# A mixture-of-experts layer on one core: the sum in two tensors of half the columns, and gate and up weights with two rows to a partition

## The chip, the cores and the metric

The kernel runs on one core of a Trainium2 chip. The metric is the device time of one execution in microseconds (us). The core's engines work side by side, each through its own instructions in order, and wait for each other by semaphores: TensorE (PE; its weight loads are listed apart as PEld), VectorE (DVE), ScalarE (ACT), GpSimd (POOL) and SyncE (SP, which here issues DMAs). Sixteen DMA engines move data between DRAM and the on-chip memory SBUF; TensorE writes its results to PSUM.

## The reference

One decoder layer for 1024 tokens of width 1024: sparse attention and a chunked gMLP side by side, merged, projected and added to the input, and then a mixture of 32 experts. Only the last part bears on the change:

```python
# comb[t, e]: weight of expert e for token t, two experts of one group per token
y = jnp.zeros_like(h)
for e in range(N_EXPERTS):
    he = jax.nn.silu(h @ w_gate[e]) * (h @ w_up[e])     # 1024 -> 256, twice
    y = y + comb[:, e:e + 1] * (he @ w_down[e])         # 256 -> 1024
```

The result is the residual plus `y`, normalised by its root mean square and scaled by `final_norm_g`. All data are float32.

## The kernel before

Up to some 815 us the kernel normalises, projects, attends, merges (`merge`) and routes. The merged residual is written to the DRAM tensor `acc` of 1024 x 1024 floats, in pieces of 128 rows and 512 columns (L1046); the normalised tokens go to the DRAM tensor `h2d`.

The mixture of experts runs over 28 units, in an order fixed when the program is built. Six experts have a fixed place, the others are ordered by their load at run time. A unit is one expert, with up to 128 tokens (three heavily loaded ones have a second, half-size list in the same unit), or a duo: two lightly loaded experts with 64 tokens each. For each unit:

- GpSimd gathers its tokens from `h2d` (L1472) into one of three SBUF pages, whose tiles are called `h` and `g` in the trace: one token on a partition, 1024 columns.
- TensorE transposes them in eight pieces of 128 columns (L1488 in `tokens`, L1500 in `tokens_duo`; output `xt`). The gathered rows are the stationary operand, the identity is the moving one. ScalarE copies the result out (`xh` or, for a duo, `xs`); for a unit that isn't a duo VectorE computes the low part `xl`.
- TensorE multiplies with gate and up weights, eight pieces of 128 rows with gate and up side by side in 512 columns (`gate_up`, L148 to L150 and L1567, L1568; `gate_up_duo`, L1514; output `gu`). A unit that isn't a duo has its weights split into a high part (`wh`, ScalarE, L135) and a low part (`wl`, VectorE, L143) and takes three products per piece.
- ScalarE and VectorE make the activation (`kb`), TensorE multiplies with the down weights (output `y` in PSUM, two slots), ScalarE scales it by the routing weight into one of three SBUF pages `y` (L1553).
- GpSimd issues an indirect DMA that adds the page's rows to the tokens' rows of `acc` in DRAM (`scatter`, L1618). There are 31 of these, two for a duo or a unit with a second list. All write the same tensor, so each waits until the one before has landed. The page `y` is free for ScalarE when its scatters have landed.

The last two units, both duos, aren't scattered; their `y` stays in SBUF, and in `finish` TensorE adds it to the output rows by one-hot matrices (`fin`, L1792). Ahead of that, `fg`, the scale of the last norm, is loaded by GpSimd's queue (L1703), held back until the down product of a given unit is issued on TensorE.

Weights come in pages of 512 KB through SyncE's queue: gate and up as two loads of 256 KB per page (L197, in `gu` of the plan), down as one of 512 KB (L203). They are issued ahead of use as pages come free. The order of instructions on each engine is set by the program's scheduler, from the order in the code, data dependences and its own cost model.

`finish` loads `acc` in eight pages `xf` of 128 rows (L1769), adds the kept `fin` (VectorE, L1820 and L1824; for two of the eight TensorE, L1814), squares and sums (ScalarE, L1825), scales (VectorE, L1784) and stores.

Of the kernel before, what the change touches and what calls it, by code (L numbers as in the profile page):

```python
# [21 lines left out]
P = 128  # L22
T = 1024
# [69 lines left out]
class Kern:  # L93
# [64 lines left out]
    def plan(self):  # L158
# [32 lines left out]
        def gu(gets, eng):  # L191
            for j, get in ((j, get) for j in range(4) for get in gets):

                def ld(t, j=j, get=get):
                    wg, wu, _ = get()
                    for z, w in enumerate((wg, wu)):
                        self.nc.sync.dma_start(t[:, :, z * 256 : (z + 1) * 256], w[j * 256 : (j + 1) * 256, :].rearrange("(k p) f -> p k f", p=P))  # L197

                W.append(([P, 2, 512], ld, eng))
# [33 lines left out]
    def expert(self, e):  # L233
        I = self.I
        return lambda: (I["w_gate"][0, e], I["w_up"][0, e], I["w_down"][0, e])

# [699 lines left out]
    def merge(self):  # L936
# [38 lines left out]
        self.acc = self.dram.tile([T, D], F32, name="acc")  # L975
# [55 lines left out]
        def rest(n):  # L1031
# [14 lines left out]
            writes.append((n, self.acc[rows, cs], x1))  # L1046
# [427 lines left out]

    def tokens(self, xg):
# [9 lines left out]
        for q in range(KT // n):  # L1485
            tp = self.ps1([P, n, m], "xt", tag="a")
            for k in range(n):
                self.lastpe = nc.tensor.transpose(tp[:, k, :], xg[:, (q * n + k) * P : (q * n + k + 1) * P], self.ident[:m, :m])  # L1488
# [4 lines left out]
    def tokens_duo(self, xg):  # L1493
# [3 lines left out]
        for q in range(2):  # L1497
            tp = self.ps1([P, 4, P], "xt", tag="a")
            for k in range(4):
                self.lastpe = nc.tensor.transpose(tp[:, k, :], xg[:, (q * 4 + k) * P : (q * 4 + k + 1) * P], self.ident)  # L1500
# [4 lines left out]
    def gate_up_duo(self, x, r, piece):  # L1505
# [3 lines left out]
        for j in range(4):  # L1509
            ws = [piece() for _ in range(2)]  # L1510
            for k in range(2):
                for z in range(2):
                    zs = slice(z * HALF, (z + 1) * HALF)
                    nc.tensor.matmul(pp[zs], lhsT=x[:, 2 * j + k, zs], rhs=ws[z][:, k, :], start=(j + k == 0), stop=(j + k == 4))  # L1514
# [41 lines left out]
    def gate_up(self, x, r, piece):  # L1556

        nc = self.nc
        pp = self.ps1([P, 512], "gu", tag="b")
        half = len(x) == 1  # L1560
        for j in range(4):
            h, l = piece()
            for k in (2 * j, 2 * j + 1):
                if half:

                    if k:
                        nc.tensor.matmul(pp[:HALF], lhsT=x[0][:, k, :HALF], rhs=l[:, k % 2, :], start=False, stop=False)  # L1567
                    nc.tensor.matmul(pp, lhsT=x[0][:, k, :], rhs=h[:, k % 2, :], start=(k == 0), stop=(k == KT - 1))  # L1568
                    if not k:
                        nc.tensor.matmul(pp[:HALF], lhsT=x[0][:, k, :HALF], rhs=l[:, k % 2, :], start=False, stop=False)  # L1570
                else:
                    self.mm3(pp, x[0][:, k, :], x[1][:, k, :], h[:, k % 2, :], l[:, k % 2, :], k == 0, k == KT - 1)
        if not half:
            return self.silu(pp, r)
        else:
            sg = self.small([P, 256], F32, "kb", bufs=self.NKB)
            rows = self.junk.bitcast(F32)
            nc.scalar.activation(rows, pp, AF.Copy, scale=r)
# [267 lines left out]
```

## Time and profile before

| | us |
|---|---|
| median of three runs | 1214.99 |
| lowest, highest | 1214.33, 1216.02 |
| the profiled execution's own time | 1214.61 |
| its span | 1212.9 |
| TensorE busy in it | 1107.7 (91%) |
| VectorE, ScalarE, GpSimd busy | 839.1, 535.4, 307.9 |

The profile is of one execution, and all stretches below are in microseconds from the start of its span. A busy share is an average over stages with different limits: the kernel's 91% on TensorE say nothing of the last 120 us, so the trace is read there by stretches, by what each engine waits for, and by the order of starts on a time line. On a time line, the bracket at a row's end gives how long the engine had been idle before and what it waited for last; no bracket means no idle time. [...]

### The profile page before, as it was taken

The numbers are of one execution on the slowest core, as the hardware profiler recorded it, in microseconds if no ns is written. First come the engines' busy times: TensorE is split into PE (matmuls) and PEld (weight loads), VectorE is DVE, ScalarE is ACT, GpSimd is POOL, SyncE is SP. The second block draws the span as 40 slices with busy tenths as digits, with TensorE's granted clock in tenths as the row PEclk, the third lists the DMA queues.
The fourth block names the chain that finished last, engine by engine and source line by source line (L and its number), as shares of the span: only waits on it lengthen the run. The fifth ranks groups of instructions, "written<-read, shape, count | busy, mean of one in ns | idle before, by whom it ended". The sixth has DMA issues, their size and how long they took to land. (4 is left out here: it accounts for less than half of the span.)

```text
span 1212.9 us, 17018 instructions
## 1 busy us (share of the span) xinstructions
PE 1107.7 (91%) x5714; PEld 875.5 (72%) x5714; DVE 839.1 (69%) x1640; ACT 535.4 (44%) x958; POOL 307.9 (25%) x339
## 2 busy tenths in 40 slices
PE   4999999998999998899999989996989999895684
PEld 3789888887888886789988878875765666573333
DVE  7534889899999997489887961366895754572015
ACT  6424651312222212478776431323885655562123
POOL 5100033340021120044431541222241712131220
PEclk9999999998999998999999999996999999998797
DMA  7301030302422220000006664787999999999835
GB/s 225 88 18 36 18 78 28 102 37 70 122 87 88 86 86 21 18 1 1 2 2 208 222 221 147 278 272 230 288 303 302 341 334 348 323 350 329 265 77 225
DMA packets 147995, 190.29 MB, mean 157 GB/s; under 512 B 16455, under 2 KB 119407, under 8 KB 147906
## 3 DMA queue, kind: packets, MB, share of 16 engines
q1 hardware_dynamic: 134226, 156.84, 39.2%
q0 software_dynamic: 8640, 20.81, 6.9%
q10 hardware_dynamic: 5040, 11.54, 2.5%
q8 instruction: 46, 0.75, 0.3%
q14 instruction: 43, 0.35, 0.1%
HBM read 165.22 MB, written 33.15 MB: 164 GB/s over the span
## 5 line engine op out<-in xcount | busy, mean ns | idle before, releaser
L143 DVE TENSOR_TENSOR wl<-wr,wh 128x1024 fp32r<-128x1024 f32 x156 | 197.1, 1284 | 35.8 <-ACT wh L135 28.0
L552 DVE TENSOR_SCALAR_CACHE_REDUCE junk<-idx,cand 128x384 bf16<-128x384 f32 (+2 forms) x198 | 187.0, 944 | 6.8 <-POOL idx L515 1.0
L148 PE MATMUL pj<-hT,wh 128*128 128x512 f32 (+1 forms) x464 | 179.5, 387 | 2.5 <-ACT wh L135 2.5
L150 PE MATMUL pj<-hT,wl 128*128 128x512 f32 (+1 forms) x464 | 178.3, 385 | 0.0
L149 PE MATMUL pj<-hT,wh 128*128 128x512 f32 (+1 forms) x464 | 177.9, 384 | 0.0
L135 ACT ACTIVATE wh<-wr 128x1024 fp32r<-128x1024 f32 x150 | 154.2, 1056 | 46.2 <-PE pj L149 28.5
L148 PEld LDWEIGHTS pj<-hT,wh 128*128 128x128 f32 x464 | 87.8, 189 | 19.9 <-ACT wh L135 2.7
L150 PEld LDWEIGHTS pj<-hT,wl 128*128 128x128 f32 x464 | 87.6, 189 | 16.8
L149 PEld LDWEIGHTS pj<-hT,wh 128*128 128x128 f32 x464 | 87.7, 189 | 16.5
L892 POOL TENSOR_SCALAR P<-P,pair 128x128 f32<-128x128 f32 (+3 forms) x64 | 47.9, 749 | 88.3 <-DVE pair L891 78.2
L717 POOL TENSOR_TENSOR yt<-yt,sb 128x1024 f32<-128x1024 f32 x8 | 20.1, 2510 | 169.0 <-ACT sb L725 169.0
L725 ACT ACTIVATE sb<-pj 128x512 f32<-128x512 f32 x32 | 19.0, 593 | 99.1 <-PE pj L150 99.1
L148 PE MATMUL gu<-wh,xh 128*128 128x512 f32 x144 | 59.7, 415 | 2.3 <-ACT wh L135 1.6
L149 PE MATMUL gu<-wl,xh 128*128 128x512 f32 x144 | 60.4, 419 | 1.5 <-DVE wl L143 1.2
L150 PE MATMUL gu<-wh,xl 128*128 128x512 f32 x144 | 58.7, 407 | 0.0
L148 PE MATMUL y<-wh,kb 128*128 128x512 f32 (+1 forms) x84 | 37.3, 444 | 19.1 <-ACT y L1553 17.9
L890 ACT ACTIVATE P<-S,pair 128x128 f32<-128x128 f32 (+3 forms) x64 | 47.5, 742 | 15.4 <-DVE pair L884 7.1
L1514 PE MATMUL gu<-wr,xs 128*64 128x512 f32 x224 | 54.2, 600 | 0.0
L512 DVE SCALAR_TENSOR_TENSOR idx<-rl,era,idx 128x384 f32<-128x384 f32 (+5 forms) x42 | 39.8, 947 | 20.1 <-ACT rl L508 18.9
L148 PE MATMUL xo<-wh,m 128*128 128x512 f32 x128 | 51.4, 402 | 2.1 <-ACT m L135 1.7
L1543 DVE SCALAR_TENSOR_TENSOR kb<-gu,era,kb 128x256 f32<-128x256 f32 x19 | 9.2, 482 | 63.8 <-ACT kb L1542 63.8
L508 ACT ACTIVATE rl<-ix 128x384 f32<-128x384 f32 (+5 forms) x48 | 35.8, 760 | 38.8 <-PE ix L503 34.9
(448 smaller groups left out, 2706.4 us busy)
## 6 DMA issues: line engine op xcount, KB each, us to landing
wr<-w_gate SPq DMA_DIRECT2D x128, 256.0 KB, 6.5
wr<-w_up SPq DMA_DIRECT2D x128, 256.0 KB, 6.4
wr<-w_down SPq DMA_DIRECT2D x64, 512.0 KB, 8.1
wr<-w_in SPq DMA_DIRECT2D x33, 512.0 KB, 4.3
x<-x SPq DMA_DIRECT2D x8, 512.0 KB, 8.0
sga<-sb ACTq DMA_DIRECT2D x8, 512.0 KB, 4.4
ybg<-yt POOLq DMA_DIRECT2D x8, 512.0 KB, 3.3
ybr<-ybg SPq DMA_DIRECT2D x8, 512.0 KB, 3.8
```

Source lines behind the costliest of these rows:

```text
L135: return nc.scalar.activation(out, src, AF.Copy)
L143: b = (self.nc.gpsimd if eng in "pq" else self.nc.vector).tensor_tensor(l, src, h.bitcast(F32), ALU.subtract)
L148: nc.tensor.matmul(out, lhsT=sh, rhs=mh, start=start, stop=False)
L149: nc.tensor.matmul(out, lhsT=sh, rhs=ml, start=False, stop=False)
L150: self.lastmm = nc.tensor.matmul(out, lhsT=sl, rhs=mh, start=False, stop=stop)
L508: nc.scalar.activation(r3, ps[:, :nch, :w], AF.Relu)
L512: nc.vector.scalar_tensor_tensor(acc, rl, wv, acc, op0=ALU.mult, op1=ALU.add)
L552: nc.vector.tensor_scalar(junk[:, : (j + 3) * P], self.idx[j + 2][:, : (j + 3) * P], cf[:, j : j + 1], None, op0=op, op1=ALU.add, accum_ou ...
L717: nc.gpsimd.tensor_tensor(yt, yt, sb, ALU.mult)
L890: nc.scalar.activation(p.rearrange("p (c w) -> p c w", c=nch), ps[:, :nch, :w], AF.Exp, bias=mx, scale=-1.0, accum_out=sm[:, 0:1])
L892: nc.gpsimd.tensor_scalar(p, p, sm[:, 1:2], 0.0, op0=ALU.mult, op1=ALU.add)
L1514: nc.tensor.matmul(pp[zs], lhsT=x[:, 2 * j + k, zs], rhs=ws[z][:, k, :], start=(j + k == 0), stop=(j + k == 4))
```

## The change

The change has two parts.

The weights of gate and up: before, piece k of the 1024 input rows were rows 128k to 128k + 127, one to a partition, so that a partition of a load held two rows of 1 KB from two places. Now partition p holds rows 8p to 8p + 7, piece k being the rows 8p + k, and one load brings rows 8p + 2j and 8p + 2j + 1, which are 2 KB in one run in DRAM and in SBUF. To match, the transposes read every eighth column of the gathered rows (`eighth`), and the gate and up matmuls read gate and up in two runs of 256 columns that don't lie side by side.

The sum: `acc` becomes two tensors of 1024 x 512, each scatter becomes two with 512 columns each, and `finish` loads 16 pieces of 256 KB in the place of 8 of 512 KB.

```diff
 # plan: gate and up pages
-                        self.nc.sync.dma_start(t[:, :, z * 256 : (z + 1) * 256], w[j * 256 : (j + 1) * 256, :].rearrange("(k p) f -> p k f", p=P))
-
-                W.append(([P, 2, 512], ld, eng))
+                        self.nc.sync.dma_start(t[:, z], self.two_rows(w, j))
+
+                W.append(([P, 2, 2, 256], ld, eng))
+    @staticmethod
+    def two_rows(w, j):
+        return w.rearrange("(p k) f -> p k f", k=KT)[:, 2 * j : 2 * j + 2, :]
 # merge
-        self.acc = self.dram.tile([T, D], F32, name="acc")
+        self.acc = [self.dram.tile([T, D // 2], F32, name="acc") for _ in range(2)]
-            writes.append((n, self.acc[rows, cs], x1))
+            writes.append((n, self.acc[c][rows, :], x1))
+    @staticmethod
+    def eighth(xg, k):
+        return xg.rearrange("s (p k) -> s k p", k=KT)[:, k, :]
 # tokens (tokens_duo alike)
-                self.lastpe = nc.tensor.transpose(tp[:, k, :], xg[:, (q * n + k) * P : (q * n + k + 1) * P], self.ident[:m, :m])
+                self.lastpe = nc.tensor.transpose(tp[:, k, :], self.eighth(xg, q * n + k), self.ident[:m, :m])
 # gate_up_duo (gate_up alike)
-                    nc.tensor.matmul(pp[zs], lhsT=x[:, 2 * j + k, zs], rhs=ws[z][:, k, :], start=(j + k == 0), stop=(j + k == 4))
+                    nc.tensor.matmul(pp[zs].rearrange("p (z f) -> p z f", z=2), lhsT=x[:, 2 * j + k, zs], rhs=ws[z][:, :, k, :], start=(j + k == 0), stop=(j + k == 4))
 # scatter
-        self.nc.gpsimd.indirect_dma_start(out=self.acc, out_offset=bass.IndirectOffsetOnAxis(ap=tok, axis=0), in_=y[: tok.shape[0]], in_offset=None, bounds_check=T - 1, oob_is_err=False, compute_op=ALU.add)
+        for c in range(2):
+            self.nc.gpsimd.indirect_dma_start(out=self.acc[c], out_offset=bass.IndirectOffsetOnAxis(ap=tok, axis=0), in_=y[: tok.shape[0], c * 512 : (c + 1) * 512], in_offset=None, bounds_check=T - 1, oob_is_err=False, compute_op=ALU.add)
 # finish
-            self.lastread = nc.sync.dma_start(x, self.acc[i * P : (i + 1) * P, :])
+            for c in range(2):
+                self.lastread = nc.sync.dma_start(x[:, c * 512 : (c + 1) * 512], self.acc[c][i * P : (i + 1) * P, :])
```

The instructions move little. On GpSimd, from the last gather to behind the load of `fg`, this is the row of before. A name in brackets is a semaphore waited for: DMASW are those of GpSimd's own DMAs, DMAHW of SyncE's; the three pages are `y_1291`, `y_1292` and `y_1293`.

```order
L1472 DMA h2_1126_6546<-h2d_6537,tokq_7718 128x1024 [waits DMASW6_49,PE_49]
L1618 DMA acc_6538<-y_1291_7840,tokp_7713 1024x1024 [waits DMASW4_49,Activation_49]
L1618 DMA acc_6538<-y_1292_7841,tok2_9075 1024x1024 [waits DMASW6_49,Activation_49]
L1618 DMA acc_6538<-y_1293_7842,tokp_7713 1024x1024 [waits DMASW7_49,DMASW0_49,Activation_49]
L1618 DMA acc_6538<-y_1291_7840,tokp_7713 1024x1024 [waits DMASW0_49,Activation_49]
L1703 DMA fg_1826_10378<-final_norm_g 128x1024 [waits DMAHW3_49,DMAHW2_49,DMAHW4_49,DMAHW0_49,DMAHW7_49,DVE_49,PE_49]
L1618 DMA acc_6538<-y_1291_7840,tokp_7713 1024x1024 [waits DMASW3_49,DMASW1_49]
```

And this is the same stretch of the changed kernel, where `acc_6538` and `acc_6539` are the two tensors:

```order
L1478 DMA h2_1126_6547<-h2d_6537,tokq_7719 128x1024 [waits PE_49]
L1631 DMA acc_6538<-y_1291_7841,tokp_7714 1024x512 [waits DMASW5_49,Activation_49]
L1631 DMA acc_6539<-y_1291_7841,tokp_7714 1024x512 [waits DMASW6_49,DMASW1_49]
L1631 DMA acc_6538<-y_1292_7842,tok2_9118 1024x512 [waits DMASW0_49,Activation_49]
L1631 DMA acc_6539<-y_1292_7842,tok2_9118 1024x512 [waits DMASW1_49]
L1631 DMA acc_6538<-y_1293_7843,tokp_7714 1024x512 [waits DMASW4_49,DMASW2_49,Activation_49]
L1631 DMA acc_6539<-y_1293_7843,tokp_7714 1024x512 [waits DMASW3_49]
L1631 DMA acc_6538<-y_1291_7841,tokp_7714 1024x512 [waits DMASW4_49,Activation_49]
L1631 DMA acc_6539<-y_1291_7841,tokp_7714 1024x512 [waits DMASW7_49,DMASW5_49]
L1716 DMA fg_1826_10466<-final_norm_g 128x1024 [waits DMAHW1_49,DMAHW6_49,DVE_49,PE_49]
L1631 DMA acc_6538<-y_1291_7841,tokp_7714 1024x512 [waits DMASW6_49]
```

Each scatter has become a pair in its place, and each half waits for the half before it of the same tensor (two issues back; a further semaphore of GpSimd's eight stands where one is used again). The load of `fg` keeps its place between two pairs.

On SyncE, two pages of gate and up in the middle of the experts, before:

```order
L197 DMA wr_1719_9866<-w_gate 128x2x256 [waits DMAHW3_49,DVE_49]
L197 ISA
L197 DMA wr_1719_9866<-w_up 128x2x256 [waits DMAHW4_49]
L245 TENSOR_LOAD eid_7582
L197 ISA
L197 DMA wr_1722_9879<-w_gate 128x2x256 [waits DMAHW5_49,PE_49]
```

and now:

```order
L197 DMA wr_1719_9939<-w_gate 128x512 [waits DMAHW3_49,PE_49]
L197 ISA
L197 DMA wr_1719_9939<-w_up 128x512 [waits DMAHW4_49]
L250 TENSOR_LOAD eid_7583
L197 ISA
L197 DMA wr_1722_9952<-w_gate 128x512 [waits DMAHW5_49,PE_49]
```

Nothing is moved here: the same loads follow each other, and a partition's share is one run of 512 elements where it was two of 256.

## Rows read from the trace of the kernel before

**Rows 1.** Stretches: us, busy time (instructions) of each engine, clock, DMA share, GB/s.

```profile
core 0: us, PE busy (x) PEld busy (x) DVE busy (x) ACT busy (x) POOL busy (x), PEclk, DMA share, GB/s
1020.00:1060.00 40.00, 35.78 (x167) 22.69 (x166) 18.02 (x23) 19.63 (x30) 8.53 (x7) 0.96 1.05 336
1060.00:1090.00 30.00, 29.32 (x145) 21.04 (x146) 22.18 (x25) 21.40 (x28) 10.93 (x7) 1.00 1.06 343
1090.00:1143.00 53.00, 31.44 (x122) 18.20 (x120) 7.15 (x10) 11.74 (x17) 9.72 (x8) 0.84 0.93 296
```

**Rows 2.** TensorE's waits, 842 to 1090 us: total us, times, longest.

```profile
PE gu L148 <- ACT wh L135: 1.6, 2, 1.2
PE gu L149 <- DVE wl L143: 1.2, 3, 0.8
```

**Rows 3.** Time line of TensorE, 1086 to 1180 us: start, duration, instruction.

```profile
1129.08 0.80 PE L148 MATMUL y<-wh,kb 128*128 128x512 f32 x1 [7.43 <-ACT y L1553]
...
1134.50 7.20 PE L1514 MATMUL gu<-wr,xs 128*64 128x512 f32 x32
1144.25 0.66 PE L1500 MATMUL xt<-identr,h 128*128 128x128 f32 x4 [2.55 <-ACT xs L1501]
```

**Rows 4.** Time line of ScalarE, 1085 to 1178 us.

```profile
1115.43 1.11 ACT L1553 ACTIVATE y<-y,ws 64x1024 f32<-64x1024 f32 x1 [5.94 <-DMA acc<-y,tokp]
1127.91 1.11 ACT L1553 ACTIVATE y<-y,era 128x1024 f32<-128x1024 f32 x1 [11.37 <-DMA acc<-y,tokp]
...
1142.60 1.11 ACT L1553 ACTIVATE y<-y,era 128x1024 f32<-128x1024 f32 x1 [6.68 <-DMA acc<-y,tok]
```

**Rows 5.** Time line of GpSimd, 1080 to 1178 us.

```profile
1088.53 1.59 POOL L1618 DMA_INDIRECT acc<-y,tokp  x1 [0.30 <-ACT y L1553]
1098.70 1.42 POOL L1618 DMA_INDIRECT acc<-y,tok  x1 [8.58 <-DMA acc<-y,tokp]
1105.92 1.61 POOL L1618 DMA_INDIRECT acc<-y,tokp  x1 [5.80 <-DMA acc<-y,tok]
1116.15 1.44 POOL L1618 DMA_INDIRECT acc<-y,tokp  x1 [8.62 <-DMA wr<-w_down]
1121.72 0.64 POOL L1703 DMA_DIRECT2D fg<-final_norm_g  x1 [4.13 <-PE y L150]
1122.66 1.49 POOL L1618 DMA_INDIRECT acc<-y,tokp  x1 [0.30 <-issue]
1128.55 1.58 POOL L1618 DMA_INDIRECT acc<-y,tokp  x1 [4.40 <-DMA acc<-y,tokp]
1135.43 1.42 POOL L1618 DMA_INDIRECT acc<-y,tok  x1 [5.31 <-issue]
1143.22 1.57 POOL L1618 DMA_INDIRECT acc<-y,tokp  x1 [6.38 <-DMA acc<-y,tok]
```

**Rows 6.** DMA issues, 1143 to 1177 us: count, KB each, median us to landing.

```profile
xf<-acc SPq DMA_DIRECT2D x1, 512.0 KB, 3.2
...
acc<-y,tok POOLq DMA_INDIRECT x1, 3.1
```

**Rows 7.** Time line of SyncE's queue, 1086 to 1180 us.

```profile
1176.99 3.25 SPq L1769 DMA_DIRECT2D xf<-acc  x7
```

**Rows 8.** Time line of VectorE, 1176 to 1213 us.

```profile
1182.94 0.69 DVE L1820 TENSOR_TENSOR xf<-fin,xf 128x512 f32<-128x512 f32 x1 [0.86 <-PE fin L1792]
```

**Rows 9.** DMA queue of SyncE, 1090 to 1143 us: packets, MB, share of 16 engines.

```profile
q1 hardware_dynamic: 10091, 13.17, 70.2%
```

**Rows 10.** The same queue, 1060 to 1090 us.

```profile
q1 hardware_dynamic: 8496, 9.12, 89.2%
```

**Rows 11.** Line L1488, 842 to 1090 us: nanoseconds min/median/max, first and last start.

```profile
L1488 PEld LDWEIGHTS xt<-identr,h x112: 133/140/230, 852.8 to 1086.2; 128*128 128x128 f32 x96, 64*128 64x128 f32 x16
L1488 PE MATMUL xt<-identr,h x112: 222/273/474, 853.0 to 1086.3; 128*128 128x128 f32 x96, 64*128 64x64 f32 x16
```

**Rows 12.** Line L1290, whose moving operand lies in three runs.

```profile
L1290 PE MATMUL list<-B,A x32: 206/235/282, 824.5 to 840.5; 128*128 128x96 bf16 x32
```

More of the change, by code (lines that the diff above doesn't have):

```diff
@@ L1499, in tokens_duo @@
             for k in range(4):
-                self.lastpe = nc.tensor.transpose(tp[:, k, :], xg[:, (q * 4 + k) * P : (q * 4 + k + 1) * P], self.ident)
+                self.lastpe = nc.tensor.transpose(tp[:, k, :], self.eighth(xg, q * 4 + k), self.ident)
             a = nc.scalar.activation(x[:, q * 4 : q * 4 + 4, :], tp, AF.Copy)
@@ L1558, in gate_up @@
         nc = self.nc
-        pp = self.ps1([P, 512], "gu", tag="b")
+        ps = self.ps1([P, 512], "gu", tag="b")
+        pp = ps.rearrange("p (z f) -> p z f", z=2)
         half = len(x) == 1
@@ L1566, in gate_up @@
                     if k:
-                        nc.tensor.matmul(pp[:HALF], lhsT=x[0][:, k, :HALF], rhs=l[:, k % 2, :], start=False, stop=False)
-                    nc.tensor.matmul(pp, lhsT=x[0][:, k, :], rhs=h[:, k % 2, :], start=(k == 0), stop=(k == KT - 1))
+                        nc.tensor.matmul(pp[:HALF], lhsT=x[0][:, k, :HALF], rhs=l[:, :, k % 2, :], start=False, stop=False)
+                    nc.tensor.matmul(pp, lhsT=x[0][:, k, :], rhs=h[:, :, k % 2, :], start=(k == 0), stop=(k == KT - 1))
                     if not k:
-                        nc.tensor.matmul(pp[:HALF], lhsT=x[0][:, k, :HALF], rhs=l[:, k % 2, :], start=False, stop=False)
+                        nc.tensor.matmul(pp[:HALF], lhsT=x[0][:, k, :HALF], rhs=l[:, :, k % 2, :], start=False, stop=False)
                 else:
-                    self.mm3(pp, x[0][:, k, :], x[1][:, k, :], h[:, k % 2, :], l[:, k % 2, :], k == 0, k == KT - 1)
+                    self.mm3(pp, x[0][:, k, :], x[1][:, k, :], h[:, :, k % 2, :], l[:, :, k % 2, :], k == 0, k == KT - 1)
         if not half:
-            return self.silu(pp, r)
+            return self.silu(ps, r)
         else:
@@ L1577, in gate_up @@
             rows = self.junk.bitcast(F32)
-            nc.scalar.activation(rows, pp, AF.Copy, scale=r)
+            nc.scalar.activation(rows, ps, AF.Copy, scale=r)
             tp = self.ps1([P, 4, HALF], "gut", tag="a")
@@ L1743, in moe @@
                     for z, w in enumerate((wg, wu)):
[L1744 removed]
+                        nc.sync.dma_start(raw.rearrange("p (z k f) -> p z k f", z=2, k=2)[:, z], self.two_rows(w, j))
                 else:
@@ L1750, in moe @@
                 if j < 4:
-                    h, l = (t.rearrange("p (k f) -> p k f", k=2) for t in (h, l))
+                    h, l = (t.rearrange("p (z k f) -> p z k f", z=2, k=2) for t in (h, l))
                 todo.append((h, l))
```

1 line of the change is left out of this document (removed).

## The prediction

> **What bounds the kernel now.** The first view is the table of stretches [rows 1]. Up to 1090 us TensorE is the bound: it is busy 29.32 of the 30 us from 1060 to 1090. The DMA engines are full there too (a share of 1.06), which looks like a second bound, so the view to read next is what TensorE waits for in the mixture of experts. Its two waits that lead back to weights are those for the high and low parts split out of a weight page, 1.6 and 1.2 us in 250 us [rows 2]; no wait for a DMA stands among its largest. So the loads are busy, but the pages come in time. After 1090 the picture turns: TensorE is busy 31.44 of 53 us [rows 1].
>
> What it waits for there is read backwards over three engines. TensorE waits for ScalarE's weighted output `y` (7.43 us in one of these waits) [rows 3]; ScalarE's `y` waits for a landed scatter, 5.94, 11.37 and 6.68 us [rows 4], since the page it writes (three in the ring) is still being read by an old scatter; and GpSimd issues a scatter when the one before has landed, because each adds into the same tensor `acc` [rows 5]. From 1088.53, the nineteenth scatter, no gather stands between them, and seven steps lead to 1143.22: 54.69 us, 7.8 us each. GpSimd works only 1.42 to 1.61 us of each step. The chain of the scatters is the bound of this stretch. It hands over at 1144.25, where TensorE transposes the last unit's input behind ScalarE's copy [rows 3]; the products of the last units and the output follow from there. What the end of the kernel gains is what this place gains.
>
> **The scatters in halves.** Each half still takes an offset for every row, so GpSimd's time doubles: a second issue of about 1.5 us and the 0.30 us that stands between two issues [rows 5], 1.8 us in all, and a pair costs 3.6 us, under the shortest step of 5.89 us. The halves depend only on halves: the first one waits for the first one of the scatter before. So a step of the chain becomes the time of a half, and the second half lands about 1.8 us behind the first. That 1.8 us is paid where both are wanted, when `y` takes the page.
>
> How much shorter is a half? A step in which little is moved is bounded by a scatter of few rows on quiet engines, which lands 3.1 us after its issue [rows 6]; with the 0.72 us from a landing (taken as the start of `y`, 1115.43) to the next issue (1116.15) that is 3.8 us. All above it can shrink by half at most, and by nothing if what counts is the number of rows. I take 0.3 of it: some is waiting behind weight packets, which halves meet as well. Steps one to three (10.17, 7.22, 10.23) stand 16.2 us above three quiet steps: 0.3 of that is 4.9. The second half of the twenty-first scatter lands 4.9 - 1.8 = 3.1 us earlier.
>
> Then comes a step that halves don't shorten. The load of `fg` stands ahead of the twenty-third scatter on GpSimd and waits for TensorE's `y` [rows 5], which waits for ScalarE's `y`, which needs both halves of the twenty-first. From 1115.43 to 1122.66 this takes 7.23 us, as long as before; without it the twenty-third's first half could start some 3 us earlier. So it starts 3.1 us earlier, and its second half (a step of 5.89, so 0.6 less) lands 3.1 + 0.6 - 1.8 = 1.9 us earlier. ScalarE's `y` of 1127.91 and TensorE's `y` and gate-up (1129.08, and 1134.50 plus 7.20) [rows 3, 4] hang on it: TensorE is through at 1141.70 - 1.9 = 1139.8. The twenty-fifth's second half lands 3.1 + 0.3 x (2.1 + 3.1 + 4.0) - 1.8 = 4.1 us earlier (the steps of 5.89, 6.88 and 7.79), `y` begins at 1138.5 and the input's copy behind it lets TensorE begin at 1140.1. TensorE is nearly as late as the scatter: the 2.55 us that it waits there now [rows 3] are almost used up. The gain is 4 us. With half of the excess instead of 0.3, the twenty-third's second half lands 8.1 - 1.8 + 1.0 - 1.8 = 5.5 us earlier, TensorE is the later one, and the gain is 5.5 + 2.55, some 8; with nothing of it each of the two places pays its 1.8 us, a loss of 3.6. The bounds are -8 and +3.6, taken -4.
>
> The rest of the pairs costs nothing in TensorE's part: before 1088 a scatter has a gather's wait for TensorE around it, and gathers are a ring of three ahead. A gather queued behind a pair starts 1.8 us later there; if its cover is gone, it costs that, once or twice. ScalarE's order swaps one `y` with one input copy near 1088, 1 to 3 us for a page that its scatter wants only 17 us later (1105.92): nothing.
>
> **The finish.** Sixteen loads instead of eight: seven issues take 3.25 us [rows 7], so 0.46 us each. The first page now ends with the fourth issue, 1.4 us later. It landed 3.2 us after 1176.99 [rows 6], VectorE wants it at 1182.94, and only after TensorE [rows 8]: 2.7 us of cover, enough for 1.4, not quite for 1.4 and 1.8 together. Zero to +1, taken 0, since the last scatters gain as well.
>
> **The loads.** Gate and up rows of 1 KB become 2 KB. Two stretches give the price of a packet: 70.2% of 16 x 53 us over 10091 packets is 59.0 ns for 1305 bytes on average, 89.2% of 16 x 30 us over 8496 packets is 50.4 ns for 1073 bytes [rows 9, 10]. The line through both has 10.6 ns per packet beside 0.037 ns per byte, an estimate. 256 loads with 256 packets each become half as many: 32768 x 10.6 / 16 = 21.7 us of engine time less. It lies beside TensorE. What can come out is what TensorE waits for weights, 1.6 + 1.2 us [rows 2], at most the 4.2 us in which it stood still from 1020 to 1060 [rows 1]. I take -2, between 0 and -4.2.
>
> **The new strides.** With rows 8p + k on a partition, the transposes read every eighth column of the gathered rows, 32 bytes apart, as stationary operand: 112 by L1488 from `h` [rows 11] and 64 more by it from `g` and by L1500 before 1090. A load takes 140 ns, a group of four transposes 0.66 us with a last one of 273 ns, so one starts each 129 ns or so [rows 3, 11], and loads run beside the matmuls before. Nothing in the trace has this stride. Taken at 0 since a load may grow somewhat under that pitch; the upper bound is a load that doubles with nothing hidden, 176 x 0.14 = 24.6 us. The matmuls of gate and up read their moving operand as two runs of 256; the nearest row reads three runs of 32, at 235 ns for 96 columns, no slower than 273 for 128 plain ones [rows 11, 12]. Zero.
>
> **The sum** is made against the profiled run, 1214.61 us (a span of 1212.9 and 1.7 around it; the median of the runs is 0.4 higher): 1214.6 - 4 - 2 = 1208.6.
>
> **Rivals.** (A) The strided load shows. From the point at which a load exceeds the pitch of 129 ns, each of 176 transposes on TensorE's bounding stretch is longer by the excess; a doubled load shown in full gives 1208.6 + 24.6 = 1233, half of it 1221. For it: no row has the stride. Against it: 140 ns of load is already pipelined under 129 ns starts, so there is slack by overlap. [...] Chance 0.12. (B) Halves don't shorten a step, as latency and the number of rows set it: 1214.6 + 3.6 - 2 = 1216.2, or 1218 if the loads bring nothing; 0.25. For it: GpSimd's 1.5 us and the quiet 3.1 us don't shrink; against it: steps vary between 5.89 and 10.23 us with what else is on the engines. (C) Both pay at their bounds, or loads that come sooner also free the crowded accumulates: -8 - 2 to -8 - 4.2, 1202.4 to 1204.6; 0.15. (D) The change doesn't do what it says, if a half had to wait for both halves before it; then 1.8 us per step, 13 more, 1225: the order shows each half waiting for one queue's half alone, chance under 0.02, counted with A.
>
> **How the numbers follow.** The forecast (1204.6 to 1212.6) has 0.46, C 0.15, B 0.25, A and D 0.14. A measurement can tell some 0.2%, 2.4 us. Faster (below 1212.6): forecast and C, 0.61. B lies on both sides of 1217.4: 0.16 of it same, 0.09 slower. With A and D slower is 0.23. The range takes in C with 1 us to spare and B with 1 us for the finish, and leaves out A: 1201 to 1219.
>
> **What would show it.** In the changed kernel's trace: transposes in groups of four still no longer than 0.66 us (else A); steps of the last scatters' first halves of 5 to 8 us, mean about 6.5 instead of 7.8, second halves issued 1.8 us behind (else B); the wait of GpSimd's `fg` load unchanged at its place; the last unit's transposes on TensorE near 1140 instead of 1144.25; packets per MB of weights fallen by nearly half and SyncE waiting less, with TensorE's busy time from 842 to 1088 the same. I am wrong if the whole shift already exists at 1088 us in either direction, since then weights or strides, and not the scatters, made it.

## The result and the profile after

| | median us | runs | ratio to before, 95% interval |
|---|---|---|---|
| before | 1214.99 | 7 | |
| changed kernel | 1221.08 | 7 | 1.0052 [1.0035, 1.0070] |
| the same again | 1223.04 | 12 | 1.0040 [1.0019, 1.0061] |
| the same, a third time | 1222.40 | 6 | 1.0041 [1.0026, 1.0057] |

The change makes the kernel 5 to 6 us slower; 1208.6 was forecast, within 1201 to 1219. The profile that came with the first measurement is of an outlying execution (1230.81 us), so "after" below is the profile of the third measurement, 1223.37 us with a span of 1221.6; of the other profiles, that of halves_only (1217.70 us) lies 3.8 us below its median and that of half_alone (1213.09 us) 5.8 us above.

Four marks cut the time into stages: TensorE's last product ahead of the experts (`xo`), the 19th scatter, the 26th, and the first `fin` product. The table is worked out from their start times in the time lines; "pinned" and "warm" are explained with the experiments.

| us | `xo` to 19th scatter | 19th to 26th | 26th to `fin` | `fin` to end | median ratio |
|---|---|---|---|---|---|
| before | 275.97 | 54.69 | 31.74 | 37.94 | 1 |
| after | 281.47 | 53.47 | 34.58 | 37.86 | 1.0041 |
| after_pinned | 276.65 | 50.33 | 35.42 | 37.86 | 0.9998 |
| halves_only | 277.97 | 51.39 | 35.76 | 37.89 | 1.0029 |
| halves_pinned | 275.90 | 51.85 | 34.74 | 37.90 | 0.9988 |
| halves_pinned_warm | 275.49 | 50.89 | 34.25 | 37.98 | 0.9973 |
| loads_only | 278.08 | 55.01 | 32.78 | 38.24 | 1.0015 |
| stride_only | 277.52 | 58.07 | 33.11 | 37.93 | 1.0057 |
| pairs | 278.00 | 53.04 | 31.76 | 38.08 | 0.9995 |

After stands 8.7 us above before: 1.7 of it lies ahead of `xo`, where the change touches nothing, 5.5 in the first stage, -1.2 in the seven steps, +2.8 behind them. The marks of before and after, from TensorE's time lines (start, duration, instruction, idle time before it; the scatters of before are in [rows 5]):

```profile
812.56 0.39 PE L150 MATMUL xo<-wh,m 128*128 128x512 f32 x1
1174.96 0.50 PE L1792 MATMUL fin<-yh,S 128*128 128x512 f32 x1 [0.44 <-ACT yh L1536]
```

```profile
814.23 0.39 PE L150 MATMUL xo<-wh,m 128*128 128x512 f32 x1
1183.75 0.51 PE L1806 MATMUL fin<-yh,S 128*128 128x512 f32 x1 [0.44 <-ACT yh L1547]
```

The first stage is the surprise. TensorE is the bound there as before [rows 1]; the stretch ahead of the 19th scatter is just as full after, and the stretch of the scatters as empty (columns as in [rows 1]):

```profile
1070.00:1097.00 27.00, 26.31 (x128) 19.16 (x127) 19.58 (x22) 17.16 (x22) 11.19 (x8) 1.00 0.88 280
1097.00:1151.00 54.00, 33.33 (x122) 19.45 (x121) 7.49 (x11) 12.59 (x18) 21.91 (x16) 0.81 0.94 297
```

Over the whole first stage TensorE is busy 4.0 us longer and idle 1.5 us longer; first before, then after:

```profile
812.56:1088.53 275.97, 251.78 (x1223) 171.16 (x1222) 186.47 (x321) 165.86 (x226) 88.45 (x70) 0.95 0.98 314
```

```profile
814.23:1095.70 281.47, 255.77 (x1223) 175.56 (x1222) 185.16 (x320) 164.66 (x225) 123.02 (x89) 0.95 0.94 308
```

The waits of TensorE from 842 to 1097 us answer to [rows 2]: that for `wh` has grown from 1.6 to 2.8 us, and two have come in. Two of before are gone, 1.1 us of `ht` for `kb` and 0.8 us of `gut` for `junk`.

```profile
PE gu L148 <- ACT wh L135: 2.8, 2, 2.4
PE gu L149 <- DVE wl L143: 1.6, 2, 0.8
PE y L148 <- ACT y L1564: 1.3, 1, 1.3
PE xt L1499 <- ACT xs L1512: 0.4, 1, 0.4
```

Why ScalarE's `wh` is late, and TensorE busy for longer, is seen in the order. Before, TensorE's transposes of one unit's second list (64 rows, `xt<-identr,g`) stood ahead of the down product `y` and of the rest of the duo's gate and up (`gu<-wr,xs`):

```profile
1025.93 1.94 PE L1514 MATMUL gu<-wr,xs 128*64 128x512 f32 x8
1028.82 1.94 PE L1514 MATMUL gu<-wr,xs 128*64 128x512 f32 x8
1031.06 0.71 PE L1488 MATMUL xt<-identr,g 64*128 64x64 f32 x8
1034.69 3.65 PE L1514 MATMUL gu<-wr,xs 128*64 128x512 f32 x16
1041.13 0.50 PE L148 MATMUL gu<-wh,xh 128*128 128x512 f32 x1 [1.21 <-ACT wh L135]
1055.39 0.44 PE L148 MATMUL y<-wh,kb 128*64 128x512 f32 x1
```

After, the same transposes come behind `y` and behind part of the gate and up, which is cut into more runs. The wait for `wh` is then 2.35 us long, and a later `y` finds its slot in PSUM not yet emptied:

```profile
1029.92 2.79 PE L1525 MATMUL gu<-wr,xs 128*64 128x512 f32 x10
1033.29 1.93 PE L1525 MATMUL gu<-wr,xs 128*64 128x512 f32 x6
1035.52 1.07 PE L1525 MATMUL gu<-wr,xs 128*64 128x512 f32 x2
1036.52 0.50 PE L148 MATMUL y<-wh,kb 128*128 128x512 f32 x1
1039.52 1.93 PE L1525 MATMUL gu<-wr,xs 128*64 128x512 f32 x6
1041.38 1.10 PE L1499 MATMUL xt<-identr,g 64*128 64x64 f32 x8
1042.41 1.94 PE L1525 MATMUL gu<-wr,xs 128*64 128x512 f32 x8
1046.70 0.51 PE L148 MATMUL gu<-wh,xh 128*128 128x512 f32 x1 [2.35 <-ACT wh L135]
1061.17 0.44 PE L148 MATMUL y<-wh,kb 128*64 128x512 f32 x1 [1.34 <-ACT y L1564]
```

Against before the 2.35 us are no loss by themselves: there TensorE stood idle at this place for 1.14 us ahead of `ht` (1039.49) and for 1.21 us ahead of `gu`, as long in all. New are the 1.34 us and 0.5 us ahead of `wl`.

The busy time is lost in the duo's gate and up. Its 16 products show as 32 rows and belong in pairs, one product for each of the two experts (`z` in `gate_up_duo`): a run of 6 rows takes as long as one of 8 (1.93 and 1.94 us), and 2 rows alone take 1.07 us. Where the order cuts through a pair here, each part takes about the time of a pair (0.91 us, four rows of the 16 in 3.65 us). Before, the runs have 8, 8 and 16 rows and take 7.53 us; after, 10, 6, 2, 6 and 8 rows take 9.66 us, with two pairs cut. These 2.1 us are in each of the six profiles with this order. With the idle time of 1.5 us and the 1.5 to 2.1 us that kernels with the strides and the old order lose in this stage (below), they account for the 5.5 us.

ScalarE's time line of after says who carries the delay. It takes its work in order. Its copy `xh` waits 8.58 us for those transposes, and the splits `wh` that stand behind it in its queue begin only then, and at once, so they waited for nothing else:

```profile
1042.57 0.60 ACT L135 ACTIVATE xh<-xt 128x512 fp32r<-128x512 f32 x1 [8.58 <-PE xt L1499]
1043.07 1.99 ACT L135 ACTIVATE wh<-wr 128x1024 fp32r<-128x1024 f32 x2
```

The program's scheduler made this order of its own when each scatter became two instructions: from some 1017 us on, the orders of before and after differ in 59 rows of TensorE and 31 of ScalarE. The diff says nothing of it, and "The instructions move little", in the section on the change, holds for GpSimd and SyncE alone.

GpSimd's time line of the next stage answers to [rows 5]. The pairs are as forecast, 1.7 to 1.9 us apart at first, but the second halves fall back to 3.3 and 3.4 us behind theirs (1139.41 and 1142.70, 1149.17 and 1152.55):

```profile
1095.70 1.59 POOL L1631 DMA_INDIRECT acc<-y,tokp  x1 [0.30 <-ACT wh L135]
1097.59 1.56 POOL L1631 DMA_INDIRECT acc<-y,tokp  x1 [0.31 <-issue]
1105.55 1.42 POOL L1631 DMA_INDIRECT acc<-y,tok  x1 [6.39 <-DMA acc<-y,tokp]
...
1127.52 0.64 POOL L1716 DMA_DIRECT2D fg<-final_norm_g  x1 [2.57 <-PE y L150]
...
1139.41 1.42 POOL L1631 DMA_INDIRECT acc<-y,tok  x1 [2.02 <-DMA acc<-y,tokp]
1142.70 1.42 POOL L1631 DMA_INDIRECT acc<-y,tok  x1 [1.87 <-DMA acc<-y,tokp]
1149.17 1.57 POOL L1631 DMA_INDIRECT acc<-y,tokp  x1 [5.04 <-DMA acc<-y,tok]
```

The handover is late by that much. `y` needs the page whole, so it waits for the second half, and TensorE's transposes of the last unit start 3.40 us behind the 26th scatter (before: 1144.25 - 1143.22 = 1.03 us [rows 3, 5]), after a wait of 5.24 us in place of 2.55:

```profile
1150.91 1.11 ACT L1564 ACTIVATE y<-y,era 128x1024 f32<-128x1024 f32 x1 [7.26 <-DMA acc<-y,tok]
```

```profile
1152.57 1.12 PE L1511 MATMUL xt<-identr,h 128*128 128x128 f32 x4 [5.24 <-ACT xs L1512]
```

### The profile page after: what moved, and what is told of

Its sections match the earlier page's. It is cut to its first block, busy times and chain, and to the rows that moved or that the text cites. A ratio compares the mean times of both kernels' runs of the same rounds, so it can differ in the third digit from the quotient of the medians.

```text
span 1229.1 us, 17104 instructions
## 1 busy us (share of the span) xinstructions
PE 1117.0 (91%) x5714; PEld 882.0 (72%) x5714; DVE 844.9 (69%) x1640; ACT 535.4 (44%) x958; POOL 360.9 (29%) x370
## 5 line engine op out<-in xcount | busy, mean ns | idle before, releaser
L1631 POOL DMA_INDIRECT acc<-y,tokp x44 | 72.8, 1655 | 41.7 <-DMA acc<-y,tokp 21.3
```

The source lines that it names most:

```text
L1631: self.nc.gpsimd.indirect_dma_start(out=self.acc[c], out_offset=bass.IndirectOffsetOnAxis(ap=tok, axis=0), in_=y[: tok.shape[0], c * 512 : ...
```

## The experiments

Before was run beside each set on the same chip; its medians there were 1217.51 us (first four of the runs below), 1216.26 (next four), 1216.88 (next four) and 1216.68 (last four).

**The change unchanged** (again).

> The changed kernel unchanged, for a second profile: the first profiled execution took 1230.8 us, where the other runs lie near 1221, and lost some 5 us between 200 and 400 us, ahead of everything that the change touches. Expected: 1220 to 1222 us, ratio to the kernel before 1.005, and a profile near the median in which the loss stands after 820 us.

Measured: 1223.04 us, 1.0040 [1.0019, 1.0061]. Its stages (281.46, 51.82, 35.48, 37.90) agree with those of after in the first stage within 0.01 us, so the 5.5 us there are no accident of one execution.

**Halves alone** (halves_only): the diff's parts `merge`, `scatter` and `finish`, with the old loads and transposes.

```diff
-        self.nc.gpsimd.indirect_dma_start(out=self.acc, ..., in_=y[: tok.shape[0]], ...)
+        for c in range(2):
+            self.nc.gpsimd.indirect_dma_start(out=self.acc[c], ..., in_=y[: tok.shape[0], c * 512 : (c + 1) * 512], ...)
```

> The sum in two tensors by halves of the columns, with the weights loaded as before. Theory H (the halved scatters and the sixteen loads at the end make the loss): near 1221 us. Theory L (the loads, and what their layout does to TensorE's operands, make it, and the halves gain a little as the steps of the last scatters suggest, 52.1 us for seven against 54.7): 1211 to 1213 us. The forecast's own term for this part was -4, 1211 us.

Measured: 1221.49 us, 1.0029 [1.0008, 1.0051]. The halves alone lose most of what the whole change loses. The seven steps are 3.3 us shorter, the wait behind them 4.0 us longer, and the first stage is 2.0 us longer though nothing in it was meant to change: TensorE's order is the one of after, to the row.

**Loads alone** (loads_only): the other part of the diff, one tensor.

```diff
-                        self.nc.sync.dma_start(t[:, :, z * 256 : (z + 1) * 256], w[j * 256 : (j + 1) * 256, :].rearrange("(k p) f -> p k f", p=P))
+                        self.nc.sync.dma_start(t[:, z], self.two_rows(w, j))
```

> Gate and up with two rows to a partition, transposes with a step of eight columns, gate and up read in two runs, and one tensor for the sum as before. Theory H: 1213 to 1215 us, no loss. Theory L: 1221 to 1224 us, since the loss of 6 us, and what the halves gain, must come from here.

Measured: 1219.17 us, 1.0015 [0.9990, 1.0039]; no difference that these runs can tell, and the order is that of before, to the row.

**The rows alone** (stride_only): rows 8p + k and the strided transposes, but the page laid out as before, so that each run stays 1 KB.

```diff
-                        self.nc.sync.dma_start(t[:, :, z * 256 : (z + 1) * 256], w[j * 256 : (j + 1) * 256, :].rearrange("(k p) f -> p k f", p=P))
+                        self.nc.sync.dma_start(t[:, :, z * 256 : (z + 1) * 256], w.rearrange("(p k) f -> p k f", k=KT)[:, 2 * j : 2 * j + 2, :])
```

> Rows 8p + k on a partition and the transposes with a step of eight columns, but the page laid out as before: weights still arrive in runs of 1 KB, gate and up side by side in one run of 512 for TensorE; one tensor for the sum. If the loss comes from the strided weight load of the transposes: slower than before by 4 us or more, as loads_only. If it comes from the operand in two runs or from how loads arrive: 1214 to 1216 us here, and the loss in loads_only alone. The 64-row transposes start every 111 ns instead of 62 in the changed kernel; 24 of them are 1.2 us at most.

Measured: 1224.59 us, 1.0057 [1.0033, 1.0081]. In the first stage it is 1.5 us longer (loads_only 2.1). The rest of its loss is in the seven steps, 58.07 us in place of 54.69, with the same scatters; why they are slower beside 1 KB runs taken from every eighth row was not settled.

**Neighbouring rows** (pairs): rows 256j + 2p + k, so that the runs are 2 KB and the transposes read every second column instead of every eighth; one tensor.

```diff
-        return w.rearrange("(p k) f -> p k f", k=KT)[:, 2 * j : 2 * j + 2, :]
+        return w[j * 256 : (j + 1) * 256, :].rearrange("(p k) f -> p k f", k=2)
-        return xg.rearrange("s (p k) -> s k p", k=KT)[:, k, :]
+        return xg[:, (k // 2) * 256 : (k // 2 + 1) * 256].rearrange("s (p k) -> s k p", k=2)[:, k % 2, :]
```

> loads_only with another assignment of rows: page j holds rows 256j to 256j + 255, partition p the rows 256j + 2p and 256j + 2p + 1. Weights still arrive as runs of 2 KB, gate and up are still read in two runs, but the transposes read every second column (8 bytes apart) instead of every eighth (32 bytes). Theory S (the 32-byte step costs the 5 us by which stride_only is slower, the 2 KB runs give 4 us): the transposes' weight load back at 140 ns, the 64-row transposes back at 62 ns, and 4 us faster than before. Theory M (what the stride costs in time comes from the order of rows in DRAM or from chance in the last stretch, not from the load): as loads_only, 0 to 2 us slower than before, even if the load is back at 140 ns.

Measured: 1215.55 us, 0.9995 [0.9986, 1.0004]: no difference. The transposes by line answer to [rows 11] (nanoseconds, minimum, median and maximum); first after, then pairs:

```profile
L1499 PE MATMUL xt<-identr,h x118: 270/274/479, 841.8 to 1093.5; 128*128 128x128 f32 x102, 64*128 64x64 f32 x16
L1499 PEld LDWEIGHTS xt<-identr,h x116: 182/192/231, 842.6 to 1093.4; 128*128 128x128 f32 x100, 64*128 64x128 f32 x16
```

```profile
L1499 PE MATMUL xt<-identr,h x119: 270/283/485, 841.7 to 1090.4; 128*128 128x128 f32 x103, 64*128 64x64 f32 x16
L1499 PEld LDWEIGHTS xt<-identr,h x117: 192/207/231, 841.8 to 1090.3; 128*128 128x128 f32 x101, 64*128 64x128 f32 x16
```

A load of the stationary operand takes 140 ns with neighbouring columns, 192 with every eighth and 207 with every second. Only little of it shows. A group of four transposes of 128 rows takes 0.60 to 0.71 us after. Eight of 64 rows take 1.10 us where they took 0.71 (1041.38 above and 1031.06 of before), and 1.17 us in pairs. Three such groups of eight per run make 1.2 us. So a step of 32 bytes costs the load 52 ns more, and the shorter step of 8 bytes does not set it right: it costs 67 ns more.

What the longer runs bring is in the DMA queue. The page's line of SyncE's queue, before and loads_only:

```profile
q1 hardware_dynamic: 134226, 156.84, 39.2%
```

```profile
q1 hardware_dynamic: 101458, 156.84, 38.1%
```

and the median time from issue to landing, 900 to 1090 us (count, KB each, us), before and loads_only:

```profile
wr<-w_gate SPq DMA_DIRECT2D x70, 256.0 KB, 7.7
```

```profile
wr<-w_gate SPq DMA_DIRECT2D x70, 256.0 KB, 6.6
```

The packets fall by 32768, as counted, and the pages land 1.1 us sooner. TensorE's waits for `wh` and `wl` in loads_only are 1.7 and 0.8 us (before 1.6 and 1.2 [rows 2]): pages that were in time come earlier still.

**Both, with neighbouring rows** (pairs_halves): the edit of pairs and that of halves_only together.

> The changed kernel with that assignment of rows: the halves as they are. Theory S: the halves' 3 us are left and the loads' 4 us gained, 0 to 2 us faster than before. Theory M: 3 to 5 us slower than before, as the changed kernel.

Measured: 1221.54 us, 1.0041 [1.0025, 1.0056]. The loss comes with the halves, whichever way the rows lie, and its first stage, 283.23 us, is even longer than that of after.

**One half, one quarter** (half_alone, quarter_alone): the second half of each scatter left out; then only 256 columns scattered, in a tensor of their own.

```diff
-        for c in range(2):
+        for c in range(1):
```

```diff
-        self.nc.gpsimd.indirect_dma_start(out=self.acc, ..., in_=y[: tok.shape[0]], ...)
+        self.nc.gpsimd.indirect_dma_start(out=self.accq, ..., in_=y[: tok.shape[0], :256], ...)
```

> halves_only with the second half of each scatter left out (columns 512 to 1023 of the scattered experts' sum are not added): the chain consists of first halves only, and nothing waits for a second. Seven steps of the last scatters took 54.7 us whole and 51.4 us as the first halves of pairs. If the halves' own length sets the step, and pairs cost it only by being behind each other: 46 to 48 us here, and the kernel 4 us or more faster than before. If latency sets it: 51 us, and 0 to 2 us faster than before, the second half's 1.8 us alone.

> The kernel before with a scatter of the first 256 columns alone into a tensor of 256 columns of its own (the other columns of the scattered experts' sum are not added; finish loads each page in two pieces). A step is a fixed part and a part by bytes: whole 7.8 us. If half the bytes take 0.3 of the part above 3.8 off, a quarter takes 0.45 off: 6.0 us a step, 42 us for seven. If latency sets it: 50 us for seven.

Measured: 1207.25 us, 0.9921 [0.9900, 0.9941], and 1198.79 us, 0.9859 [0.9839, 0.9878]. Bytes left out are worth time, and most of it in the first stage (272.04 us with a half and 265.29 with a quarter, against 275.97); the seven steps take 53.10 and 49.04 us, against 54.69. TensorE's order isn't that of before in these two kernels either, so what they gain can't be put down to the bytes alone. The time from issue to landing, in us, of each scatter of that stretch:

| scatter | 19th | 20th | 21st | 22nd | 23rd | 24th | 25th | 26th | mean |
|---|---|---|---|---|---|---|---|---|---|
| before | 9.4 | 6.4 | 9.5 | 6.1 | 5.2 | 6.2 | 7.1 | 9.2 | 7.4 |
| half_alone | 9.3 | 6.2 | 8.4 | 6.2 | 6.1 | 4.8 | 7.2 | 8.5 | 7.1 |
| quarter_alone | 6.7 | 6.2 | 6.8 | 6.1 | 6.7 | 3.9 | 5.8 | 7.6 | 6.2 |

Half the bytes take 4% off the mean, a quarter of them 16%, most of it off the long landings: here the width of a row sets only a small part of the landing.

**The order brought back** (halves_pinned): one line more in halves_only. It issues one step's gate and up behind that step's transposes, and with that TensorE's order is that of before again, but for 27 rows; the duo's gate and up comes in runs of 18 and 14 rows, with one pair cut.

```diff
-                    with tc.issue_after(self.lastdn.ins) if u >= n - KEPT - 1 else nullcontext():
+                    with tc.issue_after(self.lastdn.ins) if u >= n - KEPT - 1 else tc.issue_after(self.lastpe.ins) if step == 18 else nullcontext():
```

> The sum in two tensors by halves of the columns with the old loads, as in halves_only, with one line more that brings TensorE's order back to that of the kernel before from the duo at 1036 us on: the gate/up of one step is issued behind the transposes of that step, so that the 64-row transposes stand ahead of y and the duo's gate/up again (27 rows of TensorE still differ from the kernel before, against 59). Theory 1 (of what halves_only loses, about 2.5 us is the new order: transposes late, ScalarE's splits queued behind them late): the wait for ScalarE's wh in that step falls back from 2.35 to about 1.2 us and the median is 1218 to 1219.5, ratio 1.001 to 1.003. Theory 2 (the order is worth nothing; the loss is the second half of each scatter alone): the median stays at 1221 to 1222, ratio 1.003 to 1.005. Theory 3 (the order was the whole loss): 1214 to 1216, ratio under 1.000.

Measured: 1215.56 us, 0.9988 [0.9973, 1.0003], against 1.0029 of halves_only. The first stage is back at 275.90 us. What remains of the halves is -2.8 us in the steps and +3.0 behind them: nothing.

**GpSimd held** (pool_busy): before, with twelve small additions on GpSimd behind each scatter.

```diff
+        with self.tc.issue_after(sc.ins):
+            for _ in range(12):
+                self.nc.gpsimd.tensor_tensor(self.spin, self.spin, self.spin, ALU.add)
```

> The kernel before, with twelve small additions on GpSimd (128x16) behind each scatter, so that GpSimd is held after each scatter about as long as the issue of a second half holds it; one tensor, whole scatters, the order of TensorE and ScalarE word for word that of the kernel before. If GpSimd being held (the gathers and the next scatter issued later) makes the halves' loss, this loses 2 to 4 us, ratio 1.002 to 1.003, and each of the seven last steps is longer by the held time, up to 1 us each. If the loss is in the second half's own landing and in the new order, this is 0 to 1 us from before, ratio 1.000 to 1.001.

Measured: 1228.36 us, 1.0105 [1.0083, 1.0126]. The experiment missed its size: twelve additions held GpSimd for 4 to 6 us, where a second half holds it for 1.9. It shows that holding GpSimd for so long costs time with the order untouched (the first stage, which ends with a scatter issued by GpSimd, is 7.5 us longer), and says nothing of 1.9 us. In halves_pinned, with 1.9 us, that stage is no longer than before, though with a better clock (see after_pinned).

**The table load moved** (halves_warm, pairs_warm): ScalarE loads the table for the last square root (1.28 us) ahead of the last unit's `kb`, for which TensorE then waits 1.99 us. Here the load is issued behind the `yh` of the unit before.

```diff
-                        with tc.issue_after(self.lastsilu.ins):
+                        with tc.issue_after(self.lastyh.ins):
                             nc.scalar.activation(self.small([P, 1], F32, "warm", bufs=1), self.eps, AF.Sqrt)
```

> halves_only with the ScalarE table load for the square root (1.28 us) moved from ahead of the last unit's kb to behind the yh of the unit before, where ScalarE has nothing to do for 2.7 us. If the half-clock stretch over the last down products (5.35 us in place of 3.65) comes from TensorE's wait of 1.99 us for kb behind that load, the wait shrinks to about 0.7 us, the stretch goes, and the median is 2.5 to 3 us under halves_only: 1218 to 1219, ratio 1.000 to 1.002. If the stretch comes whatever the wait, only the wait's 1.3 us are gained: 1220, ratio 1.003. If ScalarE's kb is not what is waited for last there, nothing: 1221.5, ratio 1.004.

> A version to beat both: the pairs loads (rows 256j+2p+k, 2 KB runs, one tensor), with the table load for the square root moved behind the yh of the last unit but one as in halves_warm. If TensorE's wait for the last kb is on the path, it gains the load's 1.28 us, and with no half-clock stretch there to lose no more: 1213.5 to 1215, ratio 0.998 to 0.999. If the last products are bound by their weights or by the eviction of the unit before, nothing: ratio 0.9995 to 1.000, as pairs had.

Measured: 1216.93 us, 1.0003 [0.9988, 1.0017], against 1.0029 of halves_only; 1214.61 us, 0.9987 [0.9973, 1.0002], against 0.9995 of pairs, which the runs can't tell apart. In the traces TensorE's wait falls from 1.99 to 0.48 us. In halves_only's profile the sixteen rows of `y` behind that wait took 5.35 us in place of 3.65, with a mean clock of 0.76 from 1171 to 1178 us (5.35 also in again); in the four profiles with the load moved they take 3.65.

**The change with the order brought back** (after_pinned), beside the change itself on one chip (after_repeat, the "after" of this text).

> The changed kernel whole, with the one line of halves_pinned that brings TensorE's order back to that of the kernel before from 1036 us on. Theory 1 (the new order makes most of the loss): 4 to 5.5 us under after_repeat on the same chip, 1217 to 1219, ratio 1.000 to 1.002, what is left being the strided transposes. Theory 2 (the strides and the second halves make it; the order matters little with the new loads): within 1.5 us of after_repeat, ratio 1.003 to 1.005.

> The changed kernel unchanged, as the base of the others on this chip: 1221 to 1223, ratio 1.003 to 1.006, as twice before. Theory 1 and theory 2 expect the same of it.

Measured: 1216.57 us, 0.9998 [0.9985, 1.0011], and 1222.40 us, 1.0041 [1.0026, 1.0057]. One line that moves no work in or out is worth 5.8 us: as much as the change lost. The time line of after_pinned at the place shown above for before and after:

```profile
1030.87 4.51 PE L1525 MATMUL gu<-wr,xs 128*64 128x512 f32 x18
1035.67 1.10 PE L1499 MATMUL xt<-identr,g 64*128 64x64 f32 x8
1036.70 0.49 PE L148 MATMUL y<-wh,kb 128*128 128x512 f32 x1
1039.69 3.65 PE L1525 MATMUL gu<-wr,xs 128*64 128x512 f32 x14
1045.27 0.49 PE L148 MATMUL gu<-wh,xh 128*128 128x512 f32 x1
1057.67 0.45 PE L148 MATMUL y<-wh,kb 128*64 128x512 f32 x1
```

The duo's gate and up takes 8.16 us in place of 9.66. From the first `y` to the `y` in the last row it takes 20.97 us; after takes 24.65 between the same two (1036.52 and 1061.17). That is 3.7 of the 4.8 us between the two first stages. Idle time has 2.1 of it (4.48 us in after, 2.37 in after_pinned); in after, the products behind the wait of 2.35 us also ran at a low clock for some 3 us (granted 0.63 in the mean from 1047 to 1051.5 us), which cost 1.4 us. The stretch from 1020 to 1066 us shows it in the mean clock, first of after, then of after_pinned (columns as in [rows 1]); before has 0.96 there too, behind its waits of 1.14 and 1.21 us:

```profile
1020.00:1066.00 46.00, 40.80 (x184) 25.45 (x180) 18.91 (x24) 19.76 (x32) 17.02 (x12) 0.96 1.01 336
```

```profile
1020.00:1066.00 46.00, 42.25 (x204) 27.41 (x201) 22.96 (x28) 23.21 (x35) 14.52 (x11) 1.00 1.04 347
```

So the line makes a third order and not quite the old one. In the profiles of after_pinned and halves_pinned_warm the mean clock of this stretch is 1.00, and in halves_pinned no single product from 1028 to 1064 us takes over 0.50 us, where before has 0.63 and 0.80. Before has three idle gaps close together (1.14, 1.21 and 0.28 us) and then 3 us at half clock (granted 0.50 from 1043 to 1046 us), where products start 0.43 us apart in place of 0.23, a loss of 1.6 us. That after_pinned is level with before therefore doesn't show the rest of the change to be free: the strides' 1.5 to 2.1 us stand against this gain. The same line in the kernel before was not tried.

**Versions to beat both** (halves_pinned_warm, pairs_halves_pinned_warm): both edits in the halves with the old loads, and in pairs_halves.

> halves_pinned with the table load moved as in halves_warm: a version to beat both. If the two edits add (order about 5 us, table load 1 to 3 us of median): 1212.5 to 1214.5, ratio 0.996 to 0.998. If both only took the same half-clock stretch away: as halves_pinned, 1215 to 1216, ratio 0.998 to 0.999.

> pairs_halves (both parts, the 2 KB loads with two neighbouring rows) with the order brought back and the table load moved. If the 2 KB loads give the halves anything (second halves land sooner on less loaded queues): 1 to 2 us under halves_pinned_warm. If their strides cost more than that, as in the runs so far: 1 to 3 us above it, ratio 0.998 to 1.000. If the order was the whole of pairs_halves' loss: 5 us under it, ratio 0.9995.

Measured: 1213.87 us, 0.9973 [0.9961, 0.9985], and 1214.62 us, 0.9986 [0.9977, 0.9994]. The first is 2.8 us under before, of which TensorE's shorter wait for `kb` is 1.5. The load is now where ScalarE has nothing to do:

```profile
1177.13 0.69 ACT L1536 ACTIVATE yh<-y,era 128x512 fp32r<-128x512 f32 x1 [0.55 <-DVE yl L1537]
1177.83 1.28 ACT L1708 ACT_TABLE_LOAD   x1
```

```profile
1171.89 3.65 PE L1531 MATMUL y<-wr,kb 128*64 128x512 f32 x16 [0.48 <-ACT kb L1524]
```

The 2 KB loads add nothing to it.

## Why the prediction was wrong

**The step that failed** is the sentence "The rest of the pairs costs nothing in TensorE's part". It priced GpSimd's extra issue before 1088 us and looked at one swap on ScalarE, and took the order on TensorE for unchanged. The order was in reach before any run: it differs in 59 rows of TensorE, from some 1017 us on, and cuts two pairs of the duo's products, 2.1 us. In a stretch in which TensorE is busy 29.32 of 30 us [rows 1], an order is no detail. It cost 5.8 us (after_repeat against after_pinned). With the 4 us of the scatters and the 2 us of the loads, neither of which came, that makes 11.8 of the 12.5 us between 1208.6 and 1221.08. The prediction named its own sign of failure, "the whole shift already exists at 1088 us": the 19th scatter starts at 1095.70 in place of 1088.53, 7.2 of the 8.7 us (1.7 of them ahead of `xo`). But it ascribed such a shift to weights or strides beforehand; the strides make 2.1 us of it at most, and the order the larger part.

**The scatters: mechanism half right, size wrong.** The chain does shorten, and both halves are wanted at the page, as said. Of the time above 3.8 us in the first three steps, 0.3 was to go. They took 27.62 us before [rows 5], 26.10 after, 25.39 in after_pinned and 24.5 to 26.1 over all profiles with the halves, so 1.5 to 3.1 of 16.2 us went, a share of 0.09 to 0.19. The second half was put 1.8 us behind the first, the time of an issue on GpSimd. That holds for the first pairs, but a second half also waits for the second half before it, and by the 25th scatter the lag is 2.8 us in after_pinned and 3.3 in after (1.8 to 3.7 over all profiles with the halves). With the smaller share and the larger lag the two cancel: in after_pinned the seven steps give 4.4 us and the stage behind them takes 3.7. Rival B, in which latency and rows set a step, comes nearest: half_alone and quarter_alone show that bytes count for little. Its time, 1.6 to 3.4 us above before, is not far from after_pinned, which is level with before; what it lacked is the order.

**The `fg` step** was forecast to keep its 7.23 us. It took 5.17 after and 5.39 in after_pinned (from ScalarE's `y` to the next scatter), by way of the clock. TensorE's twelve products of `y` in that step were busy 5.05 us before, at a mean clock of 0.57 and behind a wait of 5.93 us, and 3.00 us after, at 1.00 and behind a wait of 1.67. The two stretches, before and after:

```profile
1116.00:1122.00 6.00, 5.05 (x12) 2.53 (x12) 2.68 (x3) 0.54 (x1) 1.72 (x2) 0.57 0.83 263
```

```profile
1123.00:1128.00 5.00, 3.00 (x12) 1.54 (x12) 1.99 (x3) 1.11 (x1) 2.13 (x3) 1.00 0.84 296
```

So up to 2 of the 4.4 us that the steps gave in after_pinned are the clock's. The halves may have a part in it: the wait is 0.99 to 3.53 us in the profiles with them and 3.51 to 5.93 us in those with whole scatters and the old order.

**The loads** were to bring 2 us. The packets fell as counted, but TensorE's waits for weight pages stayed at 2.5 us of 2.8, so the term is 0. The price of a packet was too high as well: 32768 fewer took SyncE's queue from 39.2% of 1212.9 us to 38.1% of 1215.3, 12 us per engine and not 21.7.

**The strides** were taken at 0 with 24.6 as bound. Rival A's premise holds, the load is dearer (192 ns in place of 140); its price is 1.2 us in the 64-row transposes, and 1.5 to 2.1 us in the first stage of the three kernels with the strides and the old order (276 against 277.5 to 278.1), a difference that the medians of loads_only and pairs do not confirm. The count of 176 also leaves out the 12 transposes that L1500 makes from `h` ahead of 1090 us; the bound is 26.3 us.

**The finish** was right in its time: 37.9 us from the first `fin` to the end, before and after. Its working was not: the first page ends with the second issue and not the fourth, and the sixteen issues took 11.21 us, where the eight took 3.74.

**What bounds the kernel**, and where the chain hands over, was right too: after waits at the same two places.

## What to carry to other kernels

Where a scheduler orders the work, compare the order of the bounding engine in full before pricing an edit, with the tiles' numbers taken out of the names so that rows can be matched; an edit on a side engine can move that order in a stretch that it doesn't mean to change. Look for waits, and also for products that run in pairs and are cut apart: no wait shows those (here 9.66 us in place of 7.53). When an edit loses in a place that it doesn't touch, bring the order back by one dependence and measure again before blaming the edit. And cutting a chained transfer in two helps only if its time goes with its bytes: here the landing times of one run with half the bytes would have told (7.1 us in the mean against 7.4).

## What the runs showed of the hardware

An indirect DMA that adds rows into DRAM, beside a busy weight stream, lands after 7.4 us in the mean with 4 KB rows, 7.1 with 2 KB and 6.2 with 1 KB (eight scatters each). A float32 stationary operand read with a step takes longer to load at every step tried: 140 ns with none, 192 at 32 bytes and, not expected, 207 at 8 bytes. Of products on 128x64 tiles, 16 rows in one run took 3.65 us, 0.46 us for two rows, but two rows alone 1.07 us. TensorE's granted clock fell to half for some 3 us at a time behind idle time of a few us (0.50 from 1043 to 1046 us of before, the mean of 0.57 behind 5.93 us above, the 5.35 us behind 2.00 us in halves_only), but not behind each such wait: after and before show 3.65 us behind 1.99. So in these cases a stall cost 1.4 to 2 us more than it lasted, and whether it did changed with the order; what decides it was not tried.
